# Giving the sampled tokens' PSUM tiles to attention's ring of banks in a hybrid decoder step

## The chip, the cores and the metric

The kernel runs on one core of a Trainium2 chip. The metric is device microseconds (us) of one execution of the whole program, lower being better. A profile of one execution comes with a trace of every instruction: PE is TensorE's matmuls, PEld its weight loads, DVE VectorE, ACT ScalarE, POOL GpSimd and SP the engine that issues most DMAs. A line such as L1056 is line 1056 of the kernel before.

## The reference, cut to what matters

One decoder layer is computed for 1024 prompt tokens and for eight sampled tokens that share the weights.

```python
h = rms_norm(x) @ w_in                       # q, k, v, indexer, conv inputs, z, 16 tiles of merge gates
o_a = attend(q, k, v, iq, ik, iw)            # 256 best keys per query; softmax; p @ v
o_b, s_new = gated_delta_chunked(...)        # recurrent state per head
o_b = rms_norm(o_b) * silu(z)
x = x + sum_b(sigmoid(gate_b) * (o_b @ w_branch[b])) @ w_out
x = x + swiglu(rms_norm(x))
# prompt: dsa_prompt over its own keys
# sampled: dsa_sample over 1024 cached keys (pages gathered by page_table) + the new one,
#          and one step of the recurrence on state_delta
```

## The kernel before

The code is written against a framework that records instructions, and a scheduler then puts each engine's instructions into a fixed order: it walks a modelled clock, takes the earliest instruction in program order that is ready, and fills holes with later ones that are ready too. A tile comes from a pool; tiles with one tag share a fixed number of buffers, which are handed out in program order, so a tile of a tag waits until the buffer of an earlier tile of the same tag is free. PSUM has eight banks, and one such tile takes one bank.

The part in question is `attention` (L905). Prompt attention runs over eight query blocks (`ATT`, largest first) and two key groups, so 16 units. `att_scores` makes four heads' scores of one unit: two transposes of q (L267, copied out at L269 by ACT and L270 by DVE), score matmuls (L1024, L1025) whose masked result DVE reads from PSUM (L1026), then the exponential (L1031, ACT), a reciprocal (L1037, DVE) and the division (L1039 on ACT, L1041 on DVE). `att_out` transposes the probabilities (L1056), splits them into two parts (L187 on ACT, L188 on DVE, tiles `ph` and `pl`), multiplies by v (L1060, L1061, tile `PV`) and copies the result out (L1066 ACT, L1067 DVE). Scores, q transposes and probability transposes all take tiles of tag `PT`. `weave` writes the scores of a unit between the steps of `att_out` of the unit before.

After the 16 units the program writes, in this order:

- the last seven tiles of the merge gates (`gate_steps`; L163 to L165 into tile `pj`, evacuated by ACT at L863), woven with `sample_delta`, the recurrence step of the sampled tokens. That one starts with two small matmuls (L1458, L1459), an inverse square root on DVE (L196 to L200), 64 matmuls of two columns against the states (L1482, states loaded by DMA at L1436), then three small matmuls and transposes (L1493 to L1495), and eight rounds of: DVE builds `sum` (L1517), PE multiplies it (L1521), DVE adds it to the states (L1524, four per round), a DMA stores them (L1525). Its output for the sampled tokens goes to DRAM tensor `d_ob`.
- `merge_b`: `load_split` reads all of `d_ob` in twelve DMAs through two buffers `ldr` (L967), ACT and DVE split them into tiles `o` (L187, L188), and 24 groups of twelve matmuls `pj<-o` follow (L163 to L165), each evacuated by DVE (L878). Woven with it is `sample_attend`: gathers of cached keys and values by POOL (tile `kvg`, L1246), transposes (L1346), matmuls with q (L1358), a softmax, transposes of it (L1389, L1396) and matmuls with the gathered values (L1402, L1406).

Both sampled parts take their PSUM tiles from `ptq`, at these lines:

```python
ps, end_ps = self.pool("fillers", space=PSUM)
self.pq = self.pf = ps
self.pj_bufs = 1
def ptq(self):
    return self.pq.tile([128, 4, 128], F32, name="tq", tag="tq", bufs=1)
def pT(self):
    return self.ps.tile([128, 4, 128], F32, name="PT", tag="PT", bufs=5)
```

So of the eight banks `pj` has one, `tq` one, `PT` five and `PV` one. Afterwards come the rest of `merge_b`, `merge_a` (matmuls `pj<-oa`), `w_out` (matmuls `pj<-yhi`) and the feed-forward part.

Of the kernel before, what the change touches and what calls it, by code (L numbers as in the profile page):

```python
# [9 lines left out]
F32 = mybir.dt.float32  # L10
# [23 lines left out]
def weave(a, n, b=iter(()), m=0):  # L34

    x = 0
    for j, _ in enumerate(a):
        while x < m and x * n <= j * m:
            next(b, None)
            x += 1  # L40
    for _ in b:
        pass
# [12 lines left out]
class K:  # L55
# [849 lines left out]
    def attention(self, end_x):  # L905
        nc, I = self.nc, self.I
        ps, end_ps = self.pool("fillers", space=PSUM)
        self.pq = self.pf = ps
        self.pj_bufs = 1
        self.ps, end_pa = self.pool("att", space=PSUM)  # L910
        self.ap, end_a = self.pool("att")
        self.sd, end_sd = self.pool("sampled")
        last, last_n = iter(()), 0
        for i in ATT:
            for g in range(2):
                P = [None] * 4
                weave(self.att_scores(i, g, P), 13, last, last_n)
                last, last_n = self.att_out(i, g, P), i + 2
        weave(last, last_n)
        gates = list(self.gates)  # L920
        weave(self.gate_steps(gates), 5 * len(gates), self.sample_delta(), 13)
        end_x()
        end_sd()
        mg, end_mg = self.pool("mergeg")
        self.wk, self.end_sa = self.pool("sample", side="right")
        mp, end_m = self.pool("mergeb", side="right")
        steps = self.merge_b(self.load_split(mp, self.d_ob), mg)
        self.sample = self.sample_attend(mg)
        weave(islice(self.sample, 33), 25, islice(steps, BESIDE), BESIDE)
        end_pa()  # L930
        end_ps()
        self.pj_bufs, self.tp_bufs = 5, 2
        self.open_psum("ps5")
        self.pf, self.end_pf = self.pool("psm", space=PSUM)
        self.stage = self.sp.tile([128, 2048], F32, name="rs", tag="kvb", bufs=1)
        x0 = self.sp.tile([128, 4224], F32, name="x20", tag="S", bufs=1)
        self.x2h = [x0[:, 0:4 * T].rearrange("p (j t) -> p j t", j=4)]
        self.x_T(0)
        self.pq = self.ps
        for _ in steps:  # L940
            pass
        end_m()
        end_mg()
        end_a()
# [27 lines left out]
        return self.pT().rearrange("p a b -> p (a b)")  # L972

    def pT(self):
        return self.ps.tile([128, 4, 128], F32, name="PT", tag="PT", bufs=5)

    def pv(self):
        return self.ps.tile([128, 512], F32, name="PV", tag="PV", bufs=1)
# [883 lines left out]
```

## Time and profile before

| | us |
|---|---|
| median of three timed runs | 1775.06 |
| lowest and highest of them | 1770.65, 1778.87 |
| the profiled execution, its own time | 1773.84 |
| its span, first to last instruction | 1771.8 |

The span is what all windows and start times below refer to; 2.0 us of the profiled execution's own time lie around it. "Busy" of an engine is the time that its instructions cover. A matmul's recorded end is modelled, and matmuls overlap each other in the pipeline, so PE's busy time counts some waiting as work; PEld is the time that weight loads cover.

### The profile page before, as it was taken

To read this page: it belongs to the slowest core of one execution; us is meant where nothing else is said; L and a number is where in the kernel's file an instruction comes from. 1 tells how busy PE (TensorE), PEld (TensorE's weight loads), DVE (VectorE), ACT (ScalarE), POOL (GpSimd) and SP (SyncE) were. 2 spreads that over 40 slices of the span, in tenths; PEclk is the share of its full clock that TensorE was granted. 3 is DMA by queue.
4 is the path that set the end of the run, shared out by engine and by line. 5 is a ranking of instruction groups with operands and counts; after the bars stand their busy time and mean duration, and the time that the engine had idled before them with its cause. 6 is when DMAs were issued, how large, how long until landed. Compare 5 with 4: busy or idle time off the path is not lost.

```text
span 1771.8 us, 31786 instructions
## 1 busy us (share of the span) xinstructions
PE 1721.3 (97%) x12300; PEld 1662.9 (94%) x12300; DVE 1214.9 (69%) x2809; ACT 847.1 (48%) x1575; POOL 30.4 (2%) x61
## 2 busy tenths in 40 slices
PE   6999999999999999999899999999999999999998
PEld 5998989999999989979898999999999999999998
DVE  7676658999799868799856488776666665733322
ACT  5566467777835436687534254443333333412112
POOL 0001100000000000000000000000000000000000
PEclk9999999999999999999999999999999999999999
DMA  6015434433645543354667444332222223722122
GB/s 209 30 38 159 127 101 137 147 97 114 175 127 160 174 144 95 111 166 144 220 203 237 141 128 138 102 108 85 72 85 84 79 78 128 236 68 81 45 81 69
DMA packets 293595, 218.02 MB, mean 123 GB/s; under 512 B 39292, under 2 KB 267456, under 8 KB 292412
## 3 DMA queue, kind: packets, MB, share of 16 engines
q1 hardware_dynamic: 291716, 205.50, 38.2%
q0 software_dynamic: 1728, 10.49, 1.7%
q8 instruction: 97, 1.59, 0.4%
q14 instruction: 54, 0.44, 0.1%
HBM read 154.17 MB, written 61.87 MB: 122 GB/s over the span
## 4 chain that ended last, share of the span: by engine, by line
PE 85%; DMA 6%; DVE 4%; ACT 3%; issue 2%; SPq 0%; POOL 0%; ACTq 0%; DVEq 0%; POOLq 0%
PE pj L163 15%; PE pj L165 15%; PE pj L164 15%; PE F L1734 2%; PE F L1736 2%; PE F L1735 2%; PE A L1734 2%; PE A L1735 2%; PE A L1736 2%; PE D L1734 2%; PE D L1736 2%; PE D L1735 2%; PE PT L1056 2%; PE B L1735 1%; PE B L1734 1%
## 5 line engine op out<-in xcount | busy, mean ns | idle before, releaser
L163 PE MATMUL pj<-xhi,whi 128*128 128x344 f32 x912 | 297.9, 327 | 5.2 <-ACT gs L863 4.3
L165 PE MATMUL pj<-xhi,wlo 128*128 128x344 f32 x912 | 293.7, 322 | 0.0
L164 PE MATMUL pj<-xlo,whi 128*128 128x344 f32 x912 | 292.9, 321 | 0.0
L187 ACT ACTIVATE whi<-wraw 128x1024 fp32r<-128x1024 f32 (+4 forms) x126 | 115.2, 914 | 245.4 <-PE pj L164 197.5
L163 PEld LDWEIGHTS pj<-xhi,whi 128*128 128x128 f32 x912 | 171.8, 188 | 9.5 <-ACT gs L863 5.6
L164 PEld LDWEIGHTS pj<-xlo,whi 128*128 128x128 f32 x912 | 171.7, 188 | 2.5 <-issue 1.1
L165 PEld LDWEIGHTS pj<-xhi,wlo 128*128 128x128 f32 x912 | 171.7, 188 | 1.2
L164 PE MATMUL pj<-act,whi 128*128 128x344 f32 x528 | 170.2, 322 | 0.0
L163 PE MATMUL pj<-act,whi 128*128 128x344 f32 x528 | 169.9, 322 | 0.0
L165 PE MATMUL pj<-act,wlo 128*128 128x344 f32 x528 | 168.8, 320 | 0.7 <-DVE wlo L188 0.7
L188 DVE TENSOR_TENSOR wlo<-wraw,whi 128x1024 fp32r<-128x1024 f32 (+3 forms) x104 | 116.4, 1119 | 48.2 <-ACT whi L187 47.3
L1798 DVE TENSOR_TENSOR x<-pj,x 128x344 f32<-128x344 f32 x96 | 48.7, 514 | 142.4 <-PE pj L165 142.4
L769 DVE TENSOR_SCALAR_CACHE_REDUCE kvb<-S,cand 128x384 bf16<-128x384 f32 (+3 forms) x128 | 103.7, 810 | 2.0
L165 PEld LDWEIGHTS pj<-act,wlo 128*128 128x128 f32 x528 | 99.3, 188 | 1.0 <-DVE wlo L188 1.0
L163 PEld LDWEIGHTS pj<-act,whi 128*128 128x128 f32 x528 | 99.3, 188 | 0.6
L164 PEld LDWEIGHTS pj<-act,whi 128*128 128x128 f32 x528 | 99.3, 188 | 0.0
L1735 PE MATMUL A<-hb,wlo 128*128 128x258 f32 x328 | 92.6, 283 | 0.0
L1734 PE MATMUL A<-hb,wlo 128*128 128x258 f32 x328 | 92.5, 282 | 0.0
L1736 PE MATMUL A<-hb,wlo 128*128 128x258 f32 x328 | 92.3, 282 | 0.0
L1734 PE MATMUL D<-hb,wx 128*128 128x258 f32 x308 | 87.1, 283 | 0.0
L1735 PE MATMUL D<-hb,wx 128*128 128x258 f32 x308 | 87.0, 282 | 0.0
L1736 PE MATMUL D<-hb,wx 128*128 128x258 f32 x308 | 87.0, 283 | 0.0
(604 smaller groups left out, 4785.8 us busy)
## 6 DMA issues: line engine op xcount, KB each, us to landing
wraw<-in_w_gate_up SPq DMA_DIRECT2D x50, 512.0 KB
wraw<-in_w_in SPq DMA_DIRECT2D x38, 512.0 KB
d_act<-x SPq DMA_DIRECT2D x41, 258.0 KB
araw<-d_act SPq DMA_DIRECT2D x20, 516.0 KB
d_g<-gs SPq DMA_DIRECT2D x48, 172.0 KB
wraw<-in_w_out SPq DMA_DIRECT2D x16, 512.0 KB
wraw<-in_w_branch SPq DMA_DIRECT2D x12, 512.0 KB
wraw<-in_w_down SPq DMA_DIRECT2D x16, 384.0 KB
```

What stands on the lines that cost most here:

```text
L163: nc.tensor.matmul(ps, lh, rh, start=(j == 0), stop=False)
L164: nc.tensor.matmul(ps, lh, rl, start=False, stop=False)
L165: nc.tensor.matmul(ps, ll, rh, start=False, stop=(j == last))
L187: self.nc.scalar.activation(hi, src, AF.Copy)
L188: self.nc.vector.tensor_tensor(lo, src, hi.bitcast(F32), op=ALU.subtract)
L769: nc.vector.tensor_scalar(junk[:r, :n], s, thr[:r, j:j + 1], 0.0, op0=ALU.is_lt, op1=ALU.add, accum_out=cnt[:r, j:j + 1])
L1056: nc.tensor.transpose(p[:, j, :], P[j][:, 128 * s:128 * s + 128], self.ident)
L1734: nc.tensor.matmul(p, lh, rh, start=(first and k == 0), stop=False, skip_group_check=True)
L1735: nc.tensor.matmul(p, lh, rl, start=False, stop=False, skip_group_check=True)
L1736: nc.tensor.matmul(p, ll, rh, start=False, stop=(k == 3), skip_group_check=True)
L1798: nc.vector.tensor_tensor(xv, p, xv, op=ALU.add)
```

## The change

`ptq` becomes `pT` from the opening of the `att` pool to its end: the sampled tokens' tiles carry tag `PT` and come from the same ring as attention's. The ring has six banks in place of five, and the bank of `tq` is gone. Two added lines move the line numbers behind them by one or two: L1024 of before is L1026 of the changed kernel, L1482 is L1484.

```diff
     def attention(self, end_x):
         nc, I = self.nc, self.I
         ps, end_ps = self.pool("fillers", space=PSUM)
-        self.pq = self.pf = ps
+        self.pf = ps
         self.pj_bufs = 1
+        self.ptq = self.pT
         self.ps, end_pa = self.pool("att", space=PSUM)
...
         end_pa()
         end_ps()
+        del self.ptq
         self.pj_bufs, self.tp_bufs = 5, 2
...
     def pT(self):
-        return self.ps.tile([128, 4, 128], F32, name="PT", tag="PT", bufs=5)
+        return self.ps.tile([128, 4, 128], F32, name="PT", tag="PT", bufs=6)
```

The scheduler makes another order of it on PE, DVE, ACT and SP; POOL's order is the same. PE at the opening of attention, where gate matmuls (`pj<-xhi`) run, in the kernel before:

```order
L1458 MATMUL tq<-ssq_8643,ones 128x96
L1459 MATMUL tq<-sgd,ones 128x64
L267 MATMUL PT<-ident,qn 128x128 x2
L1482 MATMUL tq<-skq,st 128x2 x8
L163 MATMUL pj<-xhi,whi 128x344
L164 MATMUL pj<-xlo,whi 128x344
L165 MATMUL pj<-xhi,wlo 128x344
```

The same matmuls of the sampled recurrence stand in the changed kernel among the last matmuls of the last attention unit (P, ph and pl are that unit's probabilities):

```order
L1058 MATMUL PT<-ident,P 128x128 x2
L1460 MATMUL PT<-ssq_8643,ones 128x96
L1461 MATMUL PT<-sgd,ones 128x64
L1484 MATMUL PT<-skq,st 128x2 x7
L1058 MATMUL PT<-ident,P 128x128 x2
L1484 MATMUL PT<-skq,st 128x2
L1484 MATMUL PT<-skq,S_8869 128x2 x4
L1484 MATMUL PT<-skq,S_8875 128x2 x4
L1062 MATMUL PV<-ph,v_6586 128x512
L1484 MATMUL PT<-skq,st 128x2 x4
L1063 MATMUL PV<-pl,v_6586 128x512
```

They have moved behind all 16 units but for these few rows. PE in the tenth of the units, in the second half of attention, in the kernel before (`tq<-ident,kvg` is sampled attention, `pj<-o` is `merge_b`):

```order
L1024 MATMUL PT<-k_6585,q_8060 128x512
L1025 MATMUL PT<-k_6585,q_8060 128x512
L1056 MATMUL PT<-ident,P 128x128 x4
L1346 MATMUL tq<-ident,kvg 128x128 x4
L1024 MATMUL PT<-k_6585,q_8060 128x512
L1025 MATMUL PT<-k_6585,q_8060 128x512
L1056 MATMUL PT<-ident,P 128x128 x4
L163 MATMUL pj<-o_9455,whi 128x344
L164 MATMUL pj<-o_9456,whi 128x344
L165 MATMUL pj<-o_9455,wlo 128x344
```

The same unit in the changed kernel:

```order
L1026 MATMUL PT<-k_6585,q_8060 128x512
L1027 MATMUL PT<-k_6585,q_8060 128x512
L1058 MATMUL PT<-ident,P 128x128 x4
L1063 MATMUL PV<-pl,v_6586 128x512
L1062 MATMUL PV<-ph,v_6586 128x512
L1063 MATMUL PV<-pl,v_6586 128x512
L1062 MATMUL PV<-ph,v_6586 128x512
L1026 MATMUL PT<-k_6585,q_8060 128x512
L1027 MATMUL PT<-k_6585,q_8060 128x512
L1058 MATMUL PT<-ident,P 128x128 x4
```

Between its attention matmuls nothing else is left: from the end of the gates to the last unit PE's order holds 368 attention matmuls and no other, and the first `pj<-o` comes after the last of them. SP's queue behind the last unit in the changed kernel, where `out_delta_s` are the stores of the sampled states and `ldr` the reads of `d_ob` for `merge_b`:

```order
L1513 DMA d_ob<-so 128x4x8
L1438 DMA st<-in_state_delta 128x4x128
L1527 DMA out_delta_s<-S_9199 128x4x128
L1438 DMA S_9421<-in_state_delta 128x4x128
L1527 DMA out_delta_s<-S_9300 128x4x128
L1438 DMA S_9432<-in_state_delta 128x4x128
L1527 DMA out_delta_s<-st 128x4x128 x2
L969 DMA ldr<-d_ob 128x4x86 x2
L1527 DMA out_delta_s<-S_9421 128x4x128
L1527 DMA out_delta_s<-S_9432 128x4x128
L969 DMA ldr<-d_ob 128x4x86 x2
```

In the kernel before, the first two `ldr` entries of SP's queue stand after the fourth of attention's sixteen stores of `d_oa`, and all twelve before the seventh; now all sixteen stores, the store of `so` and most stores of states are ahead of the first `ldr`.

## Rows read from the trace of the kernel before

**Rows 1.** The page, busy time of PE (share of the span, instructions).

```profile
PE   1721.3 (97%) x12300; PEld 1662.9 (94%) x12300; DVE 1214.9 (69%) x2809; ACT 847.1 (48%) x1575; POOL 30.4 (2%) x61
```

**Rows 2.** Windows: length, busy PE, PEld, DVE, ACT, POOL, PE's clock, DMA share, GB/s.

```profile
645.00:745.00 100.00, 99.95 (x639) 93.54 (x639) 83.76 (x231) 64.37 (x115) 0.00 (x0) 1.00 0.38 114
745.00:766.00 21.00, 19.00 (x109) 14.65 (x108) 18.56 (x52) 17.23 (x34) 3.94 (x5) 1.00 0.78 273
753.00:766.00 13.00, 11.52 (x70) 8.71 (x68) 12.28 (x37) 12.04 (x26) 0.00 (x0) 1.00 0.89 318
766.00:871.00 105.00, 103.83 (x682) 93.05 (x682) 95.92 (x245) 78.80 (x186) 4.39 (x5) 1.00 0.46 147
871.00:900.00 29.00, 24.52 (x167) 21.23 (x166) 14.31 (x30) 8.64 (x17) 1.27 (x2) 0.88 0.74 258
900.00:958.00 58.00, 55.63 (x375) 51.98 (x373) 38.86 (x80) 24.17 (x49) 0.00 (x0) 1.00 0.68 214
883.60:890.40 6.80, 5.25 (x18) 5.06 (x19) 2.72 (x7) 2.37 (x5) 0.00 (x0) 0.50 0.74 223
```

**Rows 3.** PE's timeline at L1458: start, duration, what runs.

```profile
645.61 0.35 PE L1458 MATMUL tq<-ssq,ones 128*128 128x96 f32 x2
```

**Rows 4.** PE's matmuls into pj, 640 to 960: ns, first and last start.

```profile
L165 PE MATMUL pj<-xhi,wlo x107: 314/320/407, 639.9 to 745.5; 128*128 128x344 f32 x107
L165 PE MATMUL pj<-o,wlo x96: 315/320/405, 770.8 to 877.7; 128*128 128x344 f32 x96
```

**Rows 5.** PE's timeline where w_out begins.

```profile
958.46 0.37 PE L163 MATMUL pj<-yhi,whi 128*128 128x258 f32 x1
```

**Rows 6.** PE's groups by line, 645 to 871: busy, mean ns, idle before.

```profile
L1056 PE MATMUL PT<-ident,P 128*128 128x128 f32 x288 | 42.9, 273 | 0.2
L1024 PE MATMUL PT<-k,q 128*128 128x512 f32 (+5 forms) x96 | 35.0, 369 | 0.8 <-DVE st L1026 0.5 <-DVE q L270 0.2
```

**Rows 7.** Windows of the instructions on sampled tiles (tq) alone.

```profile
645.00:745.00 100.00, 12.14 (x80) 10.79 (x80) 10.97 (x40) 0.94 (x4) 1.00 0.38 114
```

**Rows 8.** Windows of the instructions on PT alone.

```profile
745.00:766.00 21.00, 12.42 (x78) 10.63 (x78) 13.56 (x25) 5.98 (x11) 1.00 0.78 273
766.00:871.00 105.00, 36.99 (x223) 29.19 (x222) 49.20 (x94) 25.26 (x51) 1.00 0.46 147
```

**Rows 9.** Windows of the instructions on PV alone.

```profile
745.00:766.00 21.00, 8.55 (x21) 3.49 (x21) 1.37 (x2) 1.19 (x2) 1.00 0.78 273
766.00:871.00 105.00, 24.39 (x67) 11.76 (x67) 6.86 (x10) 6.42 (x11) 1.00 0.46 147
```

**Rows 10.** PE's timeline with attention nearly alone, with idle and releaser.

```profile
756.10 0.50 PE L1061 MATMUL PV<-pl,v 128*128 128x512 f32 x1 [0.60 <-DVE pl L188]
...
757.97 0.50 PE L1060 MATMUL PV<-ph,v 128*128 128x512 f32 x1 [0.44 <-ACT ph L187]
```

**Rows 11.** DVE's groups by line, 745 to 871, that touch neither PT nor PV.

```profile
L1041 DVE TENSOR_SCALAR P<-P,st 128x640 f32<-128x640 f32 (+5 forms) x22 | 9.5, 435 | 0.4
...
L1026 DVE DVE_READ_ACCUMULATOR2_ANT st<- 128x1 f32 x56 | 4.6, 82 | 0.0
...
L1037 DVE RECIPROCAL st<-st 128x2 f32<-128x2 f32 x22 | 3.3, 155 | 0.3 <-ACT P L1031 0.2
```

**Rows 12.** DVE's line L1517: ns, first and last start.

```profile
L1517 DVE TENSOR_TENSOR sum<-sv,eye x8: 681/684/687, 672.0 to 726.1; 128x512 fp32r<-128x512 f32 x8
```

**Rows 13.** Timeline of one round of the recurrence.

```profile
731.07 0.40 PE L1521 MATMUL tq<-sum,sk 128*128 128x512 f32 x1
...
731.50 1.12 DVE L1524 SCALAR_TENSOR_TENSOR S<-S,sC,tq 128x128 f32<-128x128 f32 x4
```

**Rows 14.** SP's timeline, two loads of states.

```profile
651.02 3.57 SPq L1436 DMA_DIRECT2D S<-in_state_delta  x2
```

**Rows 15.** SP's timeline, eight of the twelve ldr loads.

```profile
770.04 5.99 SPq L967 DMA_DIRECT2D ldr<-d_ob  x4
...
780.50 5.86 SPq L967 DMA_DIRECT2D ldr<-d_ob  x4
```

## Prediction

> **What bounds the kernel now.** I read the page first, then busy time by window, then the groups and the timeline around the change. The page shows PE busy nearly all the time [rows 1], but that is a mean over stages, so the windows decide. The part that the change touches runs from L1458 at 645.6 us [rows 3] to the first matmul of w_out at 958.5 [rows 5]: 313 us. Inside it lie three kinds of stretch. From 645 to 745, attention runs beside gates and the recurrence, and from 766 to 871 beside merge_b and sampled attention; PE is busy without a hole in both [rows 2]. Between 745 and 766 the gates have ended (745.5) and merge_b has not begun (769.6 to 770.8 by its lines) [rows 4], so attention is almost alone. There PE falls behind: from 753 to 766 the weight loads cover 8.71 of 13 us, while DVE is busy for 12.28 and ACT for 12.04 [rows 2], and PE's waits end on `pl` from DVE and `ph` from ACT [rows 10]. So attention by itself is bound by DVE and ACT, and the other work is what fills PE. What to see: PE is the bound only as long as every stretch of attention has other matmuls beside it.
>
> **The change, part by part.** Banks first, since that is what the diff edits. PE sat idle before L1056 for 0.2 us and before L1024 for 0.8 us in all of 645 to 871 [rows 6]. These are the matmuls that take a `PT` tile, so a sixth bank has at most 1.0 us to give; I count it as nothing, because PE is covered by other work there.
>
> The second effect is in the order. Slots of a tag are handed out in program order, and the sampled parts are written after the 16 units. With a tag of their own their tiles were free at once; in attention's ring they must wait for the last unit's tiles. So the recurrence moves from the first half of attention to its end, `merge_b`, which needs the recurrence's `d_ob`, moves behind it, and so does sampled attention. The gates stay. I lay the 313 us out anew, in five terms.
>
> *With gates: 92.* Before, this took 100 us (645.5 to 745.5). The 80 matmuls on `tq` go, 10.8 us of weight loads [rows 7]. A little more attention fits under the gates: the order leaves 368 attention matmuls behind them, and before there were 78 + 223 + 21 + 67 = 389 [rows 8, 9], so 21 more run here, at (29.19 + 11.76) / 290 = 0.141 us each, 3 us. Bounds 89 (the 21 for nothing) and 98 (half of the 10.8 was beside other matmuls anyway).
>
> *Attention alone: 82.* From 745 to 766 PE issued 78 + 21 = 99 attention matmuls in 21 us [rows 8, 9], 0.212 each; 368 of them take 78. I add 4 for the last unit, whose steps have no next unit beside them (chosen). Lower bound: DVE without a wait, 12.28 us for 70 matmuls [rows 2], so 65 for 368. Upper bound: DVE's work on attention for the 389 matmuls was 13.56 + 49.20 on PT, 1.37 + 6.86 on PV [rows 8, 9] and 9.5 + 4.6 + 3.3 on P and the sums [rows 11], 88.4 together, so 83.6 for 368; at DVE's busy share of 12.28 in 13 that is 88.5, with the 4 it is 93. I take 82, since the stretch it comes from is the very case. PE's weight loads would need only 14.12 / 99 × 368 = 52 us, so 30 us of PE are lost here.
>
> PE's rows allow two readings of that stretch: the matmul row says 11.52 of 13 us busy and the weight loads 8.71 [rows 2]. The Trainium skill ("Perfetto Trace Analysis", Identifying the Most-Contended Engine) holds matmul busy time for a poor measure of how near TensorE is to its limit, because matmuls are pipelined, and LDWEIGHTS time for a good one. The waits [rows 10] agree with it. By matmul records the displaced work below would come out at 123 instead of 125, and the sum 2 us lower.
>
> *Recurrence exposed: 27.* Before, it ran under PE-bound work and cost only its matmuls. Now it stands alone between attention and `merge_b`. A round is L1517 with 0.684 us on DVE [rows 12], then from PE's L1521 at 731.07 to the end of the four L1524 at 732.62, 1.55 us [rows 13]: 2.3 with the hand-off, eight rounds 18.4. Ahead of the rounds come state loads (a pair held SP's queue for 3.57 us [rows 14]), 64 tiny matmuls and a string of small DVE steps. Before, 26.4 us passed from L1458 to the first L1517 (645.6 to 672.0 [rows 3, 12]), but with DVE shared; I take a third, 8.6, as part of it falls under the last unit. Bounds: 18 if the rounds overlap so that DVE alone counts, 8 × (0.684 + 1.12) = 14.4, plus one pair of loads; 36 if two thirds of the 26.4 remain.
>
> *PE work that must follow: 125.* `merge_b`, sampled attention and `merge_a` keep PE as long as before. Weight loads from 766 to 958 cover 93.05 + 21.23 + 51.98 = 166.3 [rows 2]; attention's part of it is 29.19 + 11.76 = 41 [rows 8, 9], gone.
>
> *Idle within that: 28.* Before, 871 to 958 had 87 − 73.2 = 14 us without weight loads [rows 2]; that stays. New is `load_split`: eight of its twelve loads took from 770.04 to 786.36 [rows 15], so all twelve take 24.5 us, through two buffers. Before, attention covered them; now only the first steps of sampled attention do. I take 10 of 24.5 (bounds 0 and 24.5). And a stretch of waits cost PE its clock before: from 883.6 to 890.4 it was granted 0.50 (1.2 of 2.4 GHz), after small matmuls with gaps, and 18 matmuls took 6.8 us [rows 2], 0.38 each, where from 900 to 958 at full clock 375 took 58 us, 0.155 each; that is 4 us, and I expect it once more behind the recurrence. On SP the state loads, the stores and `ldr` now stand behind all sixteen stores of `d_oa`; none of these is waited for by PE but in the way just counted. POOL's order is unchanged, but its gathers wait for tiles that sampled attention frees later; I put that into the same bound. Bounds 14 and 42.
>
> Sum: 92 + 82 + 27 + 125 + 28 = 354, against 313: 41 us more. The profiled execution took 1773.84, so 1815; the median of the three runs lies 1.2 above that execution, so 1816.
>
> **The rivals.** *Little is exposed.* The rounds overlap (18 for 27) and sampled attention covers the loads (17 for 28): 92 + 82 + 18 + 125 + 17 = 334, 21 more, about 1796. For it: sampled attention needs nothing from the recurrence. Against: its own tiles come from the same ring behind the recurrence's.
>
> *All bounds meet.* 98 + 93 + 36 + 125 + 42 = 394, 81 more, 1856. For it: each step in the tail is a chain across engines with little beside it. Against: the pace of attention alone was measured.
>
> *Six banks let attention run as fast as DVE can.* PE gets further ahead with `PT` tiles, so DVE never waits, attention alone takes its 65, and the recurrence slips under the last units but for 8: 92 + 65 + 8 + 125 + 14 = 304, 9 less, about 1766. It decides once the second and third terms are under 82 together, all else at its best. The Trainium skill speaks for it ("Perfetto Trace Analysis", Matmuls): independent matmul groups should rotate through different PSUM banks, so that the emptying of one overlaps the next. In this trace DVE was already busy for 12.28 of 13 us with five banks [rows 2], and PE waited on `pl` and `ph`, which are no banks [rows 10]; that speaks against it.
>
> *The change does nothing.* The order moves, but all that is moved finds cover, and the sixth bank gives its 1.0 us: 1774. It would need 41 us of cover in a kernel whose PE has none.
>
> **How the numbers follow.** Forecast 0.60 (its own range 1802 to 1832), little exposed 0.13, all bounds 0.19, six banks 0.05, nothing 0.03. The range must lose no more than 2 in 10: I leave out the last two and about half of "all bounds", so it ends at 1846, and goes down to 1794 to hold the 1796. Faster by over 0.5% (about what a measurement of this kernel can tell from no change, 9 us) takes the six banks' case: 0.04. Within 0.5%: the rest of it and "nothing", 0.04. Slower: 0.92.
>
> **What would show it.** Right: gates end about 92 us behind the first matmul of attention's stretch; then some 80 us with PE's weight loads at two thirds and DVE above nine tenths; then some 25 us with PE nearly idle between the last `PV` and the first `pj<-o`, with the eight L1521 among them some 2.3 us apart; w_out's first matmul about 41 us later than 958.5; nothing changed behind it. Wrong: attention alone at 70 us or less, L1521 among attention's matmuls, or PE full while `ldr` loads. The forecast fails most easily on the length of the recurrence and on the clock behind it, for which the rows have only a neighbour.

## The result and the profile after

The changed kernel takes 1848.54 us in the median of three runs (1848.19 to 1851.0), against 1775.06 before: 1.0415 of it, 95% interval 1.0389 to 1.0441. That is 73.5 us slower, where 41 were forecast, and 2.5 us above the range. The profiled execution took 1848.19 us with a span of 1845.9, 74.1 us more than the span before.

The page of the changed kernel: busy time of PE, and the granted clock in 40 slices.

```profile
PE 1752.7 (95%) x12300; PEld 1678.4 (91%) x12300; DVE 1217.1 (66%) x2809; ACT 849.6 (46%) x1575; POOL 30.4 (2%) x61
...
PEclk9999999999999999985998999999999999999999
```

The work is the same, the engines' instruction counts too; what is new is a dip in the clock: 5 in the slice from 831 to 877 us, 8 in the slice before it and 8 again in the one from 969. The windows of the changed kernel (columns as in [rows 2]) cut the stretch at its own landmarks:

```profile
645.00:740.00 95.00, 93.59 (x580) 87.34 (x579) 66.30 (x157) 64.73 (x114) 0.00 (x0) 1.00 0.21 65
740.00:815.00 75.00, 63.21 (x336) 45.34 (x334) 69.38 (x195) 69.09 (x155) 3.98 (x5) 1.00 0.25 82
815.00:837.00 22.00, 19.59 (x86) 17.86 (x87) 12.29 (x51) 9.82 (x30) 0.00 (x0) 0.58 0.25 69
837.00:868.00 31.00, 11.45 (x32) 7.00 (x32) 18.77 (x65) 1.47 (x6) 0.00 (x0) 0.50 0.60 169
868.00:877.00 9.00, 4.75 (x20) 3.50 (x21) 3.88 (x9) 2.68 (x5) 0.00 (x0) 0.50 0.77 230
877.00:971.00 94.00, 87.27 (x583) 76.59 (x581) 41.41 (x74) 19.70 (x34) 5.66 (x6) 0.97 0.46 155
971.00:1038.00 67.00, 59.13 (x358) 56.39 (x357) 41.80 (x88) 30.32 (x63) 0.00 (x0) 0.90 0.81 267
```

The landmarks are the last copy of attention and the first and last matmuls into `pj`. From the changed kernel's line L1069 (L1067 of before) and its tile `pj`; ns min/median/max, then first and last start:

```profile
L1069 DVE TENSOR_TENSOR oT<-PV,pvt x16: 671/689/696, 686.1 to 837.0; 64x512 f32<-64x512 f32 x16
```

```profile
L165 PE MATMUL pj<-xhi,wlo x107: 313/320/408, 640.1 to 740.4; 128*128 128x344 f32 x107
L163 PE MATMUL pj<-o,whi x96: 316/321/634, 876.7 to 967.9; 128*128 128x344 f32 x96
L163 PE MATMUL pj<-oa,whi x96: 316/322/652, 971.4 to 1037.2; 128*128 128x344 f32 x96
L163 PE MATMUL pj<-yhi,whi x34: 279/283/385, 1037.9 to 1049.9; 128*128 128x258 f32 x34
```

Beside [rows 4, 5] the reader sees: the gates end at 740 instead of 745; `merge_b`, which ran from 770 to 878, runs from 877 to 968; `w_out` begins at 1037.9 instead of 958.5, 79.4 us later. Of these, 5 come back behind it: the first L1798, at 1510.4 before and 1586.6 now (L1800), is 76 later, the end of the span 74.

Between attention and `merge_b`, PE's timeline in the changed kernel (three of its rows):

```profile
837.66 3.55 PE L1484 MATMUL PT<-skq,S 128*128 128x2 f32 x16
...
849.50 0.80 PE L1523 MATMUL PT<-sum,sk 128*128 128x512 f32 x1 [1.92 <-DVE sum L1519]
...
872.25 0.56 PE L1315 MATMUL PT<-ident,sP 8*128 8x8 f32 x4 [5.87 <-DMA sP<-d_q]
```

The recurrence's state matmuls go by at 0.22 us each (16 in 3.55), at half clock; before, they ran inside attention, at the full one [rows 2]. Each round waits about 1.9 us for `sum`; then PE waits 5.87 us for a load of sampled attention. The chain that ended last shows what follows, in the changed kernel:

```profile
863.52 3.89 DMA ldr<-d_ob
...
870.02 2.10 DMA sP<-d_q
...
960.86 2.67 DMA d_y<-gt
963.54 4.51 DMA gt<-d_g
```

Loads stand on the chain twice: `ldr` and `sP` ahead of `merge_b`, and at its end a store of `gt` and the load into the same buffer.

### The profile page after: what moved, and what is told of

Its sections match the earlier page's. It is cut to its first block, busy times and chain, and to the rows that moved or that the text cites. A ratio compares the mean times of both kernels' runs of the same rounds, so it can differ in the third digit from the quotient of the medians.

```text
span 1845.9 us, 31819 instructions
## 1 busy us (share of the span) xinstructions
PE 1752.7 (95%) x12300; PEld 1678.4 (91%) x12300; DVE 1217.1 (66%) x2809; ACT 849.6 (46%) x1575; POOL 30.4 (2%) x61
## 4 chain that ended last, share of the span: by engine, by line
PE 82%; DMA 7%; DVE 6%; ACT 3%; issue 2%; SPq 1%; POOL 0%; ACTq 0%; DVEq 0%; POOLq 0%
PE pj L163 15%; PE pj L165 15%; PE pj L164 15%; PE F L1736 2%; PE F L1738 2%; PE F L1737 2%; PE A L1736 2%; PE A L1737 2%; PE A L1738 2%; PE D L1736 2%; PE D L1738 2%; PE D L1737 2%; DMA gt<-d_g 1%; PE B L1737 1%; PE B L1736 1%
## 5 line engine op out<-in xcount | busy, mean ns | idle before, releaser
L1800 DVE TENSOR_TENSOR x<-pj,x 128x344 f32<-128x344 f32 x96 | 48.7, 515 | 142.6 <-PE pj L165 142.6
```

The costliest lines, as they stand in the source:

```text
L1800: nc.vector.tensor_tensor(xv, p, xv, op=ALU.add)
```

## The experiments

Ratios are to the kernel before, run on the same chip, with 95% intervals. Fourteen runs followed, one of them the changed kernel once more. Of each edit only the lines that matter are shown; the first two edits are shown against the changed kernel, and they also set its ring to five banks.

**Which part carries the loss.** First, only sampled attention in the ring (five banks), the recurrence on its own bank as before.

```diff
-        self.pf = ps
+        self.pq = self.pf = ps
         self.pj_bufs = 1
-        self.ptq = self.pT
...
         weave(self.gate_steps(gates), 5 * len(gates), self.sample_delta(), 13)
+        self.ptq = self.pT
```

> The recurrence keeps a bank of its own, sampled attention alone takes tiles from attention's ring, which has five banks. Theory (the loss hangs on the recurrence coming late, since merge_b needs its d_ob): the recurrence stands in the first half of attention again, merge_b fills the second half, and only sampled attention's chain is behind attention: 1780 to 1805 us. Rival (it is sampled attention's late chain that costs most): over 1825.

Measured 1802.77 us, 1.0144 (1.0115 to 1.0173): 28 us slower than before, inside the theory's bounds. The first matmuls of its groups in `merge_b`:

```profile
L163 PE MATMUL pj<-o,whi x96: 316/320/488, 776.4 to 927.2; 128*128 128x344 f32 x96
```

`merge_b` begins at 776 again, under attention, but ends at 927, not 878, since its last groups wait behind sampled attention. Then the reverse: sampled attention on its own bank, the recurrence in the ring of five.

```diff
-        self.pf = ps
+        self.pq = self.pf = ps
         self.ptq = self.pT
...
         weave(self.gate_steps(gates), 5 * len(gates), self.sample_delta(), 13)
+        del self.ptq
```

> The reverse: sampled attention has a bank of its own, the recurrence takes tiles from attention's ring of five. Theory: the recurrence alone carries the loss, since merge_b needs d_ob and sampled attention's SBUF pool takes the room that the recurrence gives back: 1835 to 1855 us. Rival (the loss is split between the two parts by their work): about 1810.

Measured 1859.59 us, 1.0474 (1.0447 to 1.0501), 85 us, 5 above the theory's bounds and far from the rival. With a free bank sampled attention still starts behind attention: the first transposes of its gathered keys come at 883 us. Last, from the kernel before, a single tile of the recurrence in the ring:

```diff
-        p = flat(self.ptq())
+        p = flat(self.pT())
         nc.tensor.matmul(p[:, 0:96], self.ones, flat(sq), start=True, stop=True)
```

> The kernel before with one edit: of all sampled tiles only the recurrence's first one, of L1458 and L1459, comes from attention's ring; the ring has five banks and all other sampled tiles the bank of their own. Theory (one slot behind the last unit's is enough, since the rest of the recurrence, d_ob, the SBUF room and so merge_b and sampled attention hang on it): 1835 to 1860 us, as with the whole recurrence in the ring. Rival (the loss grows with the number of tiles in the ring): under 1800.

Measured 1857.82 us, 1.0463 (1.0444 to 1.0483). From its tile `pj`:

```profile
L163 PE MATMUL pj<-o,whi x96: 314/320/655, 874.1 to 949.4; 128*128 128x344 f32 x96
```

One slot that is handed out behind the last unit's puts `merge_b` at 874, as the whole change does. So the loss is an order, and the recurrence is its head; the number of tiles in the ring hardly matters.

**What a bank is worth.** The change with five banks, one left empty:

```diff
-        return self.ps.tile([128, 4, 128], F32, name="PT", tag="PT", bufs=6)
+        return self.ps.tile([128, 4, 128], F32, name="PT", tag="PT", bufs=5)
```

> The change with a ring of five banks instead of six, one bank left empty. Theory (order, not banks): same as with six within 0.5%, 1840 to 1857 us. Rival (the sixth bank gives attention something that the order hides): over 1865.

And the kernel before with four (`bufs=5` becomes `bufs=4`):

> The kernel before with four banks for attention instead of five, one left empty. Theory (banks were not the limit, PE waited 1.0 us before the matmuls that take them): within 1% of 1775, and so the sixth could not bring more than some us either. Rival (each bank is worth 1% or more): over 1793.

Five banks gave 1861.21 us, 1.0478 (1.0452 to 1.0505), above the theory's bound and below the rival's. Four gave 1790.2, 1.0088 (1.0061 to 1.0114), inside the theory's one per cent, but clear of no change. The end of attention in the kernel before, in it with four banks, and in the change with five:

```profile
L1067 DVE TENSOR_TENSOR oT<-PV,pvt x16: 673/689/695, 688.8 to 871.1; 64x512 f32<-64x512 f32 x16
```

```profile
L1067 DVE TENSOR_TENSOR oT<-PV,pvt x16: 671/690/696, 694.4 to 891.6; 64x512 f32<-64x512 f32 x16
```

```profile
L1069 DVE TENSOR_TENSOR oT<-PV,pvt x16: 673/688/695, 691.4 to 841.4; 64x512 f32<-64x512 f32 x16
```

A bank less costs the kernel before 15 us and ends its attention 20 us later; the change with six is some 10 us faster than with five. Both theories were too low: PE's idle time before the matmuls that take a `PT` tile, 1.0 us [rows 6], does not tell what a bank is worth, probably because the fixed order has put other work there. Which work the missing bank delayed was not taken apart.

**The clock.** Extra matmuls into the free bank of the ring of five, read by nobody, in two forms.

```diff
+            for _ in range(3 if i < 5 else 0):
+                nc.tensor.matmul(self.fill, self.v2[:, s, g, :], ph, start=True, stop=True)
...
+        for j in range(32):
+            nc.tensor.transpose(self.fill[:, 0:128], S0[:, j % 4, :], self.ident)
...
+                for _ in range(7 if c < 28 else 28):
+                    nc.tensor.matmul(self.fill, k4, flat(um), start=True, stop=True)
```

> The changed kernel with a ring of five, and the free bank takes extra matmuls that nobody reads (3 beside each of the last 30 steps of att_out, 32 transposes behind the recurrence's state matmuls, 7 beside each of its rounds, 28 in the last one). They add PE work and take nothing away. Theory (part of the loss is PE at half clock from 815 to 880 us, on the chain of the last units and of the recurrence): the granted clock stays at 1.00 there, L1523 takes 0.40 us again, and the time falls by 8 to 20 us against the ring of five. Rival (the clock is a symptom, DVE and the loads set this stretch): no gain, or slower by the added work, up to 20 us.

Measured 1868.83 us, 1.0509 (1.0477 to 1.0541), no faster than the ring of five (1.0478). Its windows, the tail of attention and two pieces of the rounds:

```profile
815.00:840.00 25.00, 23.07 (x136) 19.31 (x135) 18.49 (x71) 15.89 (x48) 0.00 (x0) 0.91 0.27 74
862.00:866.00 4.00, 3.22 (x9) 2.02 (x8) 1.81 (x5) 0.00 (x0) 0.00 (x0) 0.50 0.45 132
874.00:878.00 4.00, 3.22 (x15) 2.23 (x13) 2.76 (x9) 0.00 (x0) 0.00 (x0) 1.00 0.52 131
```

The first of these windows in the ring of five without extra matmuls:

```profile
815.00:840.00 25.00, 21.20 (x89) 17.69 (x89) 15.44 (x62) 12.08 (x38) 0.00 (x0) 0.63 0.23 63
```

In attention's tail the clock stayed at 0.91, against 0.63 in the ring of five, and attention ended within 2 us of it; a gain, if there was one, went into the extras. In the rounds the extras read the tile that the next round overwrites, and so lengthened them. The second form mended that:

```diff
+            for _ in range(6 if i < 2 else 0):
+                nc.tensor.matmul(self.fill, self.v2[:, s, g, :], ph, start=True, stop=True)
...
+                for _ in range(20):
+                    nc.tensor.matmul(self.fill[:, 0:128], k4, k4, start=True, stop=True)
```

> Mended form of the first try with extra matmuls, whose extras read the tile that the next round had to overwrite. Ring of five; the free bank takes 6 extra matmuls beside each of the last 6 steps of att_out and 160 short ones on a tile that nobody writes again, for PE's holes between the recurrence's rounds; they add PE work. Theory (half clock lengthens each round, 2.67 us in the changed kernel with L1523 at 0.77 us): rounds of 2.2 to 2.4 us with L1523 near 0.40, and 3 to 6 us less than the ring of five, so 4.4 to 4.6 per cent over before. Rival (the round is DVE's chain alone): rounds stay at 2.6 or more, no gain.

Measured 1869.81 us, 1.0529 (1.0512 to 1.0546). Its windows in the rounds:

```profile
850.00:860.00 10.00, 10.00 (x47) 9.81 (x46) 3.44 (x10) 0.00 (x0) 0.00 (x0) 0.50 0.26 71
860.00:870.00 10.00, 10.00 (x46) 9.81 (x46) 1.72 (x5) 0.00 (x0) 0.00 (x0) 0.50 0.31 90
```

PE had no hole and stayed at half clock, so the extras outlasted the holes and a round with its extras took 6.4 us. Neither time tells what the half clock costs. The trace of the first form does for a round, since its clock rose in the middle of the rounds. DVE's update of the states there, with its idle time while it waits for the round's product, in a round at 0.50 and in one at 1.00:

```profile
866.64 1.12 DVE L1533 SCALAR_TENSOR_TENSOR S<-S,sC,PT 128x128 f32<-128x128 f32 x4 [0.89 <-PE PT L1528]
...
876.73 1.12 DVE L1533 SCALAR_TENSOR_TENSOR S<-S,sC,PT 128x128 f32<-128x128 f32 x4 [0.59 <-PE PT L1528]
```

That is 0.30 us a round, 2.4 us for eight, as an estimate from these two; in the changed kernel DVE waits 0.89 to 0.95 in each of the last five rounds. What the half clock costs attention's tail, and how much of it all reaches the end, stays open.

**What holds merge_b back.** The change without the recurrence's rounds:

```diff
-                um = wk.tile([128, 4, 128], F32R, name="sum", tag="sum", bufs=1)
...
-                nc.tensor.matmul(flat(p), k4, flat(um), start=True, stop=True)
-                for j in range(4):
...
```

> The changed kernel with six banks and without the recurrence's eight rounds: sum, its matmul and the update of the states are left out, and the states are stored as they were loaded. Theory (the rounds stand exposed on the chain, 8 times 2.67 us): 17 to 22 us less than the changed kernel, about 1828 us. Rival (merge_b's loads of d_ob or sampled attention's gate the next stretch anyway): under 8 us less.

Measured 1844.19 us, 1.0384 (1.0359 to 1.0408): 4 us under the changed kernel, or 7 under its repeat below, as the rival had it. The rounds are exposed, yet they cover something nearly as long. Its chain that ended last:

```profile
847.92 4.30 DMA S<-in_state_delta
...
852.25 2.87 DMA out_delta_s<-S
...
855.13 2.91 DMA S<-in_state_delta
...
858.53 2.34 DMA d_ob<-so
...
861.30 1.56 DMA sP<-d_q
```

Loads and stores of states, with `d_ob` behind them. Whether it is SP's queue was tried by giving the second loads and the stores to GpSimd, with the rounds and without:

```diff
-                S0 = load_S(h, b0)
+                S0 = load_S(h, b0, nc.gpsimd)
...
-                nc.sync.dma_start(O['delta_s'][0, b0:b0 + 4, h]
+                nc.gpsimd.dma_start(O['delta_s'][0, b0:b0 + 4, h]
```

> The changed kernel with the second loads of the states and their stores issued by GpSimd instead of SP, so that d_ob and its reads by merge_b no longer queue behind them; the eight rounds stay. Theory (what holds merge_b back behind attention is SP's queue of state loads and stores more than the rounds): the first matmul of merge_b comes 6 to 12 us earlier than 39 us behind attention, and the time falls by 5 to 12 us against the changed kernel, ratio to before 1.034 to 1.039. Rival (the rounds on DVE and PE, or the SBUF room of the recurrence, hold merge_b back): less than 3 us, ratio 1.040 or more.

> The same queues, and the eight rounds left out (sum, its matmul and the state update; the states are stored as loaded). Theory: with neither rounds nor queue ahead of d_ob, merge_b starts 18 to 24 us behind attention and the time falls by 12 to 20 us against the changed kernel, ratio 1.030 to 1.035. Rival (loads of d_ob and sampled attention's own chain gate it): as without rounds alone, 1.037 or more.

> The changed kernel once more, as the yardstick on the same chip for the two others: 1.040 to 1.043 of before by every theory.

Measured, in this order: 1847.4 us, 1.0402 (1.0377 to 1.0428); 1846.13, 1.0387 (1.0358 to 1.0417); and the changed kernel itself 1851.23, 1.042 (1.0393 to 1.0447). The queue theory fell: both ratios are the rivals', and the gains, 4 and 5 us, lie within the intervals. The traces tell a little more. Executions differ by some us ahead of this stretch, those of the changed kernel too, so I count from the gates' last matmul (one execution each, us):

| | gates' last matmul | `merge_b`'s first, behind it | `w_out`'s first, behind it |
|---|---|---|---|
| changed kernel | 740.4 | 136.3 | 297.5 |
| the same once more | 746.3 | 137.1 | 297.1 |
| without the rounds | 745.9 | 126.6 | 290.4 |
| GpSimd's queue | 745.0 | 130.8 | 294.9 |
| GpSimd's queue, without the rounds | 744.9 | 131.0 | 292.2 |

Each edit lets `merge_b` begin 5 to 10 us earlier, and 2 to 7 us of that are left at `w_out`; the rounds are worth more than the queue. None frees more than about a quarter of the 40 us between attention's last matmul and `merge_b`. What SP waited for in the two kernels with GpSimd's queue, 838 to 880 us, in total, times and longest, with the rounds and without:

```profile
SPq L969 <- DVE o L188: 12.0, 3, 10.7
```

```profile
SPq L1309 <- DMA out_delta_s<-S: 8.2, 1, 8.2
```

With the rounds, `ldr` was issued early, but the buffers came free late, since DVE's split of them stands behind the rounds in its order. Without them, the load of `sP` waits for a store of a state: sampled attention's tiles lie in the SBUF room that the recurrence gives back. In the changed kernel itself SP's timeline shows a third case:

```profile
864.94 3.01 SPq L1527 DMA_DIRECT2D out_delta_s<-S  x2
868.55 0.96 SPq L969 DMA_DIRECT2D ldr<-d_ob  x2
869.62 0.70 SPq L1309 DMA_DIRECT2D sP<-d_q  x2
```

There the load of `sP` takes its turn behind the last stores of states, one of which waited 2.0 us for the last round, and behind two `ldr`; a wait of its own can't be seen. So it seems that each edit takes one gate away and meets the next. That the room holds sampled attention back was seen only without the rounds; neither a kernel with separate room nor one with `sP` ahead of `ldr` was tried.

**Can program order undo it?** The recurrence written between the units, two steps behind each; then sampled attention too, four steps behind each of the last seven units, with the gates and the pools of `merge_b` and sampled attention written ahead of the tenth.

```diff
+        sampled = self.sample_delta()
         last, last_n = iter(()), 0
...
+                for _ in islice(sampled, 2):
+                    pass
...
```

> The change with a ring of six, but the recurrence is written between the units, two steps behind each, so its slots are handed out among theirs; sampled attention stays behind all units. Theory (slots go by program order, so writing it earlier undoes its move): the recurrence runs among attention, merge_b fills the second half, and the time is that of the kernel with the recurrence on its own bank within 1%: 1780 to 1805 us. Rival (a shared ring lets the recurrence hold attention up): over 1825.

```diff
+                for _ in islice(sampled, 2) if n < LATE else islice(self.sample, 4):
+                    pass
...
```

> As before, and sampled attention too is written between the last seven units, four steps behind each, with the gates ahead of them. Theory: everything has cover again, so 1765 to 1785 us, level with the kernel of before; where it beats it, by no more than the 14 us that were idle behind attention. Rival (one ring in program order makes attention wait for the sampled chain): 1800 or more.

Measured 1819.93 us, 1.0238 (1.0206 to 1.0269), and 1813.59, 1.0211 (1.0173 to 1.025). The recurrence did move back and `merge_b` began at 773, but both missed their bounds by 15 us and more. The second one's end of attention and matmuls of `merge_b`:

```profile
L1074 DVE TENSOR_TENSOR oT<-PV,pvt x16: 677/688/697, 692.4 to 907.1; 64x512 f32<-64x512 f32 x16
```

```profile
L163 PE MATMUL pj<-o,whi x96: 316/320/427, 773.8 to 931.8; 128*128 128x344 f32 x96
```

Attention now ends at 907 and `merge_b` at 932. The first result lies between theory and rival, the second is the rival's, which had the sampled chain hold attention up. By which wait it would do so was not taken apart. The last one, from the kernel before, shares another ring: the sampled tiles with `pj`, two banks in turn, attention's five untouched.

```diff
-        self.pj_bufs = 1
+        self.pj_bufs = 2
+        self.ptq = lambda: self.pf.tile([128, 512], F32, name="pj", tag="pj", bufs=2).rearrange("p (a b) -> p a b", a=4)
```

> The kernel before, with the sampled tiles in one ring of two banks with pj, the tiles of gates and merge_b, in place of one bank each; attention keeps its five. Theory (sharing costs where the slots of the two users are far apart in program order, and gates and merge_b are written woven with the sampled parts): within 1% of 1775. Rival (any shared ring costs): 1800 or more.

Measured 1811.21 us, 1.0189 (1.0157 to 1.0222), the rival. Every shared ring that ran cost 28 us or more, and none of the kernels beat the one before.

## Why the prediction came out short

The direction, the mechanism and its place were right: the order, not the bank count, makes the loss (one tile is enough, shown), the recurrence is its head, `merge_b` goes behind attention, attention alone leaves more than a third of PE without weight loads. The sizes of the terms were off, all to the same side. Predicted against measured, from 645.6 us on:

| term | predicted | measured | from |
|---|---|---|---|
| with gates | 92 | 95 | gates end at 740.4 |
| attention alone | 82 | 96 | last `PV` matmul at 836.3 (835.52 + 0.77) |
| recurrence exposed | 27 | 31 | last update of states, 866.42 + 1.12 |
| what follows, work and idle | 153 | 170 | `w_out` at 1037.9 |
| sum | 354 | 392 | |

**Attention alone: 82** is the step that failed most of the five terms, by 14. I took the pace of 21 us of large units, 0.212 us a matmul, for all 368. From 740 to 815 the changed kernel issued some 330 in 75 us, 0.227 each, with DVE busy for 69.38 and ACT for 69.09 (second window above). The other price that I had worked out, DVE's own work of 88.4 us for 389 matmuls, is 0.227 as well; I used it only as the upper bound. That is 5 of the 14. The other 9 are the last units: 815 to 837 held some 38 attention matmuls, for which I had 8 + 4 us, and with them 45 of the recurrence's 64 state matmuls, 9.6 us of PE, at 0.58 of the clock; DVE, busy for 12.29 of 22 us, was not the bound there. I had foreseen the clock's fall only behind the recurrence. How these 9 split between the clock, the hand-offs and the state matmuls is open: holding the clock up there took extra matmuls, and brought no time.

One of PE's waits I had put at nothing. In the rows of before they end on `pl` and `ph`, which are no banks; in the changed kernel, from 740 to 837, most of the idle time before L1062 ends on DVE's copy out of `PV`, which has one bank:

```profile
L1062 PE MATMUL PV<-ph,v 128*128 128x512 f32 x43 | 19.8, 461 | 8.8 <-DVE oT L1069 6.0 <-ACT ph L187 2.8
```

Whether that made the stretch longer than DVE's own work does is not shown.

**What follows: 125 + 28.** Weight loads from 877 to 1038 covered 133 us, 8 more than the 125 (the clock was 0.90 in the last window), and left 161 − 133 = 28 without, the predicted number. That is luck in part: 8.6 us of PE's idle time there ended on `gt`, none on `ldr`. I had put the whole reload of `d_ob` inside these 28; the 9 us from 867.5 to 876.7, in which PE waits for `sP` and ACT and DVE for `ldr`, came on top.

**Recurrence exposed: 27.** Right in size (31; rounds of 2.67 us where 2.3 were forecast, with L1523 at 0.77 us; most of the difference is the clock, by the 0.30 us above), wrong as a price: without the rounds only 4 to 7 us were won. A term that stands on the path is not what its removal brings when another chain runs beside it.

**A sixth bank has at most 1.0 us to give** failed too: it gave some 10, in the other direction from the loss, so that without it the change would have cost 86. The forecast also had nothing change behind `w_out`, and 5 us came back there. Both came to its help by luck: it was 38 us short at `w_out`, where it had been worked out, and 33 in the time.

Of the rivals, the case in which all bounds meet (1856) came nearer than the forecast; attention alone (96 for 93) and what follows (170 for 167) even passed their upper bounds. The case of six banks did not come: DVE was as busy in attention alone as with five.

## What to carry to other kernels

Before tiles of two users go into one ring, look at where their slots fall in program order: one slot handed out behind the other user's last tile moves its whole chain there, and all that hangs on its output (on its SBUF room too, as argued here). Price an uncovered stretch by the work of the engine that will bound it, summed over its instructions, not by the pace of its easiest piece; here that closes 5 of the 14 us. Idle time before the instructions that take a buffer does not tell what a buffer is worth under a fixed order; taking one away does.

## What the runs showed of the hardware

PE without a hole is not PE at full clock: in the second run with extra matmuls it was busy, by its records, for 20 of 20 us from 850 to 870, after a stretch with holes, and was granted 0.50 throughout. At half clock the recurrence's 512-column matmul took 0.77 us, as against 0.40 [rows 13]; at full clock with gaps before it, in the first run with extra matmuls, it took 0.50.

That a bank moves the end of attention by 20 us, where PE had waited 1.0 us before the matmuls that use it, I had not expected either.
